# A two-layer encoder on one core: the pick of modulations one chunk behind its row product, the first sums in one piece, a constant loaded later

## The chip, the cores and the metric

The kernel runs on one core of a Trainium2 chip. The metric is the device time of one execution in microseconds (us), and less is better. The engines are TensorE (PE, whose weight loads are listed as PEld), VectorE (DVE), ScalarE (ACT), GpSimd (POOL) and SyncE (SP, which issues nearly all DMAs). Each works through its own queue in order, and waits on the others through semaphores.

## What is computed

A trunk of two residual layers over x of 1024 tokens x 1024 features, conditioned by a vector c, all in float32. The reference, cut to what matters here:

```
ada = silu(c) @ ada_w[l] + ada_b[l]          # 3 x 1024: shift, scale, gate
h   = rms_norm(x, norm_g[l]) * (1 + scale) + shift
x   = x + gate * mixer_l(h)

mixer 0: proj = h @ w_in -> q, k, v, g_a, x_b, g_b
         a = diff_attention(q, k, v) with
             lam = exp(sum(lp[0]*lp[1])) - exp(sum(lp[2]*lp[3])) + lam_init
         b = bidir_rglru(x_b)
         out = concat([a * silu(g_a), b * silu(g_b)]) @ w_out
mixer 1: neighbourhood attention over the token grid, 16 heads, with gate and w_out
```

After both layers comes a final RMSNorm. What matters here is small beside the rest: shift, scale and gate ("the modulations", ada above), the sum of squares and 1/sqrt of each norm, and the scalar lam.

## The kernel before

Features lie on the 128 partitions and tokens along the free axis. So an activation is 8 tiles (k = 0 to 7) of 128 x 1024, and each is worked on in two halves of 512 tokens (hf = 0, 1; HF = 512). A product with weights takes three passes in a reduced format: weight and activation are each split in a high and a low part (whi, wlo; ahi, alo or yhi, ylo), and `mm3` issues hi x hi, hi x lo, lo x hi (L204 to L206). One output chunk of `proj` is 8 k x 3 = 24 matmuls of 128 x 512 into one PSUM bank. Weight slabs of 512 KB (raw) are loaded by SP, split by ACT (whi, L187) and POOL (wlo = raw - whi, L188); slab i + 1 is split when chunk i has been issued.

**PSUM.** Pool pp has two banks, pool ps two and pool pt two. While `wide` is on, the chunks take pp, pp, ps, ps in turn. A row product (below) takes a bank of pp too.

**A norm.** ACT or DVE squares the tiles. `ss_add` multiplies a tile by a block of ones and adds up over partitions in a bank, `rstd_rows` (L388 to L394) makes 1/sqrt on DVE: rs, rr, then three rounds of three small operations. `spread` (L407) copies the result to all partitions by four matmuls (tile bc, or the bank norm0, norm1 at the start). `make_h` multiplies the tile by gain and 1/sqrt (L414), makes its high part on ACT (L415) and its low part on DVE (L416).

**The start.** The tiles xT, the first slabs and four sets of ada pieces (8 pieces of 256 KB each) come through SP's queue in one stream. `squares(hf)` loads and squares one half; `mod_first(g)` makes shift and scale of tiles 2g and 2g + 1: 32 small matmuls ("sums", L281, tile mod) over the 8 pieces, a copy of the row on ACT (L304), the pick (L306, a matmul that puts the row's numbers on partitions), then first and gain on DVE (L310, L312). `scale(hf)` runs `rstd_rows` and `spread` at high priority and copies the spread bank to SBUF (bcs, L555); `parts(g, hf)` calls make_h for two tiles, `products` multiplies them with the first three slabs. The constant lam is made in `small_constants` ahead of all this: its load (lpv, 128 x 256 float32, L504) stands third in SP's queue.

**The changeover** is the output projection of layer 0 (`out_layer(0, ...)`). Segment r0 does eight chunks for the first half of the tokens (weight slabs 24 to 31, tiles pp24_0 to pp31_0), r1 the same for the second half (pp32_1 on). Behind each chunk, `evac` on DVE adds gate x chunk to the residual tile (xh, L1149, at high priority), ACT squares it (L1154), and DVE adds the square to the running sum (sq, L1160). `tail(0)` is the norm of the first half: ssl, rs, rr, rt, spread.

Beside this run the modulations of layer 1, a generator `mod_part` per 512 of them. DVE adds up eight pieces of ada_w times c in a tile macc (L342, then seven of L344), with a yield after each. Then follow three empty yields, the row product (L378, tile mrow, by `ss_add`), ACT's copy of the row (L356), the pick (L361, held behind the last matmul issued so far) and the addition of ada_b on DVE (L366, mod1). The loop steps this generator three times behind each chunk (`after_dve`), and it runs over two parts in a row, so the second part's additions begin behind the first part's L366.

The order on each engine is that in which the code issues, apart from `high_priority` and `issue_after`, by which the scheduler places an instruction earlier, or behind a named one.

Of the kernel before, what the change touches and what calls it, by code (L numbers as in the profile page):

```python
# [15 lines left out]
ALU = mybir.AluOpType  # L16
# [81 lines left out]
def kernel(ctx, tc, xT, xTp, small, lamp, adaw, tb, w0, gw, wo0, w1, nab, wo1, out):  # L98
# [175 lines left out]
    def mod_first(g, pool, small, c32):  # L274
# [31 lines left out]
        T.matmul(pc[:, :4], row[:], pick[:], start=True, stop=True)  # L306
# [10 lines left out]
    def mod_part(l, t, part, pool, tag="ada", bufs=2, acc=None, wait=3, apart=False,  # L317
                 early=False):
# [39 lines left out]
        if apart:  # L358
            yield 0.0
# [49 lines left out]
    def make_h(l, k, hf, x, bc):  # L409

        g, b = first_mod[k] if l == 0 else (gain1[:, k:k + 1], modc[1][:, k:k + 1])
        hi = actp.tile([P, HF], F32R, tag=f"hi{k}_{hf}", name=f"ahi{k}_{hf}")
        lo = actp.tile([P, HF], F32R, tag=f"lo{k}_{hf}", name=f"alo{k}_{hf}")
        V.scalar_tensor_tensor(x, x, g, bc, ALU.mult, ALU.mult)  # L414
        A.activation(hi[:], x, AF.Identity, bias=b)  # L415
        V.scalar_tensor_tensor(lo[:], x, b, hi[:], ALU.add, ALU.subtract)  # L416
        hact[k, hf] = (hi, lo)
# [55 lines left out]
    def small_constants(lp):  # L473
# [27 lines left out]

        lpm = lp.tile([P, 2, 64], F32, tag="lpm", name="lpm", bufs=1)
# [10 lines left out]
    with tc.tile_pool(name="start", bufs=2) as stp, tc.tile_pool(name="ada0", bufs=KC) as adp:  # L513
# [12 lines left out]
        def squares(hf, on_dve, pool, tag):  # L526
# [5 lines left out]
            for k in range(KC):  # L532
                sq = stp.tile([P, HF], F32, tag="sq", name="sq", bufs=SQ)
                if k in on_dve:
                    V.tensor_tensor(sq[:], half(k, hf), half(k, hf), ALU.mult)
                else:
                    A.activation(sq[:], half(k, hf), AF.Square)
                sqs.append(sq)
                if hf == 0:
                    ss_add(ss, sq, k == 0, k == KC - 1)  # L540
# [8 lines left out]
        def scale(hf):  # L549

            with tc.high_priority():
                rr = rstd_rows(nbank[hf], D, stp)
                spread(rr, nbank[hf])
                bcs[hf] = stp.tile([P, HF], F32, tag="bcs", name="bcs")
                A.activation(bcs[hf][:], nbank[hf][:], AF.Copy)  # L555

        def parts(g, hf):
            for k in (2 * g, 2 * g + 1):
                make_h(0, k, hf, half(k, hf), bcs[hf][:])
# [39 lines left out]
        for g in range(1, KC // 2):  # L599
            if g == 1:  # L600
                with tc.issue_after(state["x"].ins):
                    mod_first(3, adp, stp, c32)
            for hf in range(2):
                parts(g, hf)
# [610 lines left out]
    with tc.tile_pool(name="bound", bufs=2) as bp:  # L1215
# [4 lines left out]
        mod = mods(NM[2], bp, bufs=4, wait=NW[2])  # L1220
# [361 lines left out]
```

## Time and profile before

| what | us |
|---|---|
| median of three runs | 1188.19 |
| lowest, highest run | 1186.65, 1191.43 |
| the profiled execution's own time | 1190.72 |
| its span in the trace | 1189.0 |
| PE busy | 1145.3 (96%) |
| DVE, ACT, POOL busy | 738.1, 560.3, 371.8 |

The busy times come from one profiled execution, on one core; they overlap, so they don't add up to the span. PE is the engine that is nearly always at work. "Granted clock" or PEclk is the share of full speed (2.4 GHz) that PE was given in a stretch; 0.50 is the lower level, 1.2 GHz. In a timeline, a row with "x8" groups eight instructions that follow each other, and the number in brackets is the idle time of that engine just before, with what ended it.

### The profile page before, as it was taken

The numbers are of one execution on the slowest core, as the hardware profiler recorded it, in microseconds if no ns is written. First come the engines' busy times: TensorE is split into PE (matmuls) and PEld (weight loads), VectorE is DVE, ScalarE is ACT, GpSimd is POOL, SyncE is SP. The second block draws the span as 40 slices with busy tenths as digits, with TensorE's granted clock in tenths as the row PEclk, the third lists the DMA queues.
The fourth block names the chain that finished last, engine by engine and source line by source line (L and its number), as shares of the span: only waits on it lengthen the run. The fifth ranks groups of instructions, "written<-read, shape, count | busy, mean of one in ns | idle before, by whom it ended". The sixth has DMA issues, their size and how long they took to land.

```text
span 1189.0 us, 19211 instructions
## 1 busy us (share of the span) xinstructions
PE 1145.3 (96%) x7232; PEld 975.3 (82%) x7232; DVE 738.1 (62%) x1422; ACT 560.3 (47%) x1029; POOL 371.8 (31%) x346
## 2 busy tenths in 40 slices
PE   5999999999999999999999999999999999999997
PEld 2788777888887888777878888988998998888896
DVE  6857959699888979778663344233434443555454
ACT  4357685475655657432442444344444434446121
POOL 2124322233333332343422433332333333316100
PEclk8999999999999999999999999999999999999998
DMA  9723131432122112485513433243453534314212
GB/s 325 240 80 125 36 140 53 142 90 78 36 87 63 32 39 71 145 283 183 185 46 123 139 111 91 85 134 110 129 172 88 162 126 117 93 35 156 98 72 71
DMA packets 85789, 136.46 MB, mean 115 GB/s; under 512 B 8000, under 2 KB 49472, under 8 KB 85696
## 3 DMA queue, kind: packets, MB, share of 16 engines
q1 hardware_dynamic: 85696, 135.23, 36.3%
q8 instruction: 57, 0.93, 0.3%
q14 instruction: 36, 0.29, 0.1%
HBM read 112.13 MB, written 16.78 MB: 108 GB/s over the span
## 4 chain that ended last, share of the span: by engine, by line
PE 74%; DVE 13%; ACT 5%; DMA 4%; issue 3%; POOL 1%; SPq 0%; DVEq 0%; POOLq 0%; ACTq 0%
PE pp L204 14%; PE pp L205 14%; PE pp L206 14%; PE no L1418 4%; PE etr L1400 3%; PE v L204 2%; PE v L206 2%; PE v L205 2%; PE n L671 2%; DVE e L1003 2%; PE atr L1033 2%; PE n L672 2%; PE s L671 1%; PE s L672 1%; DMA ada<-in_adaw_dram 1%
## 5 line engine op out<-in xcount | busy, mean ns | idle before, releaser
L204 PE MATMUL pp<-ahi,whi 128*128 128x512 f32 (+1 forms) x976 | 370.8, 380 | 2.0 <-DVE sgb L677 1.8
L206 PE MATMUL pp<-ahi,wlo 128*128 128x512 f32 (+1 forms) x976 | 367.9, 377 | 1.1 <-POOL wlo L188 1.1
L205 PE MATMUL pp<-alo,whi 128*128 128x512 f32 (+1 forms) x976 | 368.6, 378 | 0.0
L188 POOL TENSOR_TENSOR wlo<-raw,whi 128x1024 fp32r<-128x1024 f32 x80 | 197.0, 2465 | 260.9 <-ACT whi L187 242.2
L206 PEld LDWEIGHTS pp<-ahi,wlo 128*128 128x128 f32 x976 | 184.0, 189 | 35.5 <-POOL wlo L188 1.6
L204 PEld LDWEIGHTS pp<-ahi,whi 128*128 128x128 f32 x976 | 184.3, 189 | 34.8 <-DVE sgb L677 2.3
L205 PEld LDWEIGHTS pp<-alo,whi 128*128 128x128 f32 x976 | 184.3, 189 | 30.8 <-issue 0.2
L1389 POOL TENSOR_SCALAR e<-e,r 128x288 f32<-128x288 f32 (+1 forms) x128 | 71.2, 569 | 235.9 <-DVE r L1387 229.7
L187 ACT ACTIVATE whi<-raw 128x1024 fp32r<-128x1024 f32 x80 | 84.3, 1056 | 107.1 <-PE pp L205 52.7
L1007 ACT ACTIVATE e<-e,nm 128x1024 f32<-128x1024 f32 x64 | 73.6, 1151 | 46.6 <-DVE nm L1003 46.3
L1384 ACT ACTIVATE e<-e,nm 128x288 f32<-128x288 f32 (+1 forms) x128 | 72.7, 569 | 47.2 <-DVE nm L1381 40.4
L1406 DVE COPY e<-etr 96x384 f32<-96x384 f32 (+1 forms) x64 | 35.5, 554 | 94.2 <-PE etr L1400 91.5
L1381 DVE CUSTOM_DVE_ANT_0 e<-n,bias 128x288 f32<-128x288 f32 (+1 forms) x128 | 60.6, 504 | 45.5 <-PE n L672 33.0
L1404 ACT ACTIVATE e<-etr 96x384 f32<-96x384 f32 (+1 forms) x64 | 31.3, 489 | 117.8 <-DVE e L1406 117.4
L1003 DVE CUSTOM_DVE_ANT_0 e<-s,tb 128x1024 f32<-128x1024 f32 x64 | 77.3, 1218 | 6.4 <-PE s L672 4.9
L1024 POOL TENSOR_SCALAR e<-e,r 128x256 f32<-128x256 f32 x32 | 32.6, 1018 | 131.8 <-DVE r L1013 73.7
L204 PE MATMUL v<-whi,ahi 128*128 128x256 f32 x256 | 72.2, 282 | 0.0
L206 PE MATMUL v<-whi,alo 128*128 128x256 f32 x256 | 71.9, 281 | 0.0
L205 PE MATMUL v<-wlo,ahi 128*128 128x256 f32 x256 | 71.9, 281 | 0.0
L1040 ACT ACTIVATE ath<-atr 128x512 fp32r<-128x512 f32 x64 | 37.5, 596 | 39.7 <-PE atr L1033 39.4
L1400 PE MATMUL etr<-ident,e 128*96 128x128 f32 (+1 forms) x384 | 52.3, 272 | 0.5 <-POOL e L1389 0.5
L671 PE MATMUL s<-ks,qq 128*128 128x512 f32 x128 | 52.5, 410 | 0.0
(218 smaller groups left out, 2111.3 us busy)
## 6 DMA issues: line engine op xcount, KB each, us to landing
raw<-in_w_dram SPq DMA_DIRECT2D x56, 512.0 KB
ada<-in_adaw_dram SPq DMA_DIRECT2D x96, 256.0 KB
raw<-in_wo_dram SPq DMA_DIRECT2D x24, 512.0 KB
bias<-in_nab_dram SPq DMA_DIRECT2D x64, 144.0 KB
qq<-qq SPq DMA_DIRECT2D x48, 128.0 KB
bias<-in_nab_dram SPq DMA_DIRECT2D x32, 192.0 KB
xT<-in_xT_dram SPq DMA_DIRECT2D x16, 256.0 KB
vd<-vt SPq DMA_DIRECT2D x32, 128.0 KB
```

The lines of the kernel that those rows point to most:

```text
L187: A.activation(hi[:], raw[:], AF.Copy)
L188: G.tensor_tensor(lo[:], raw[:], hi[:], ALU.subtract)
L204: T.matmul(ps, lh, rh, start=start, stop=False)
L205: T.matmul(ps, lh, rl, start=False, stop=False)
L206: state["pe"] = T.matmul(ps, ll, rh, start=False, stop=stop).ins
L671: T.matmul(dst, qsel(q[m]), k, start=True, stop=False)
L1003: state["dve"] = V.tensor_tensor_reduce(out=e[:], in0=ps[:].rearrange("p a b -> p (a b)"), in1=tbt["tb"][:, o:o + S], scale=-1.0, scalar=3 ...
L1007: A.activation(e[:], e[:], AF.Exp, scale=-1.0, bias=nm[:], accum_out=sums[:, m:m + 1])
L1381: state["dve"] = V.tensor_tensor_reduce(out=e[:, m, :n], in0=ps[:, m, :n], in1=bias["now"][m][:, :n], scale=-1.0, scalar=3.0e38, op0=ALU.a ...
L1384: A.activation(e[:, m, :n], e[:, m, :n], AF.Exp, scale=-1.0, bias=nm[:, m:m + 1], accum_out=sums[:, m:m + 1])
L1389: state["pool"] = G.tensor_scalar(e[:, m, :n], e[:, m, :n], r[:, m:m + 1], 0.0, ALU.mult, ALU.add).ins
L1400: T.transpose(pt[:kn, m, j * P:(j + 1) * P], e[:, m, j * kn:(j + 1) * kn], ident[:])
```

## The change

Five edits, one at the changeover and four at the start:

1. `mod_part` gets `gap`, a number of empty yields between ACT's copy of the row and the pick. The modulations at the changeover use gap=3, which is one chunk's worth of steps.
2. At the start, the spread of the first half is issued behind the first pick (`state["picked"]`), so the 32 first sums stand in front of it.
3. The constant lam moves to a function of its own, `lam_constant`, called behind the loads of the fourth set of ada pieces.
4. make_h for the first two tiles of each half reads 1/sqrt from the spread's PSUM bank (`nbank`) in place of the SBUF copy bcs.
5. The squares of the second half are issued behind the last alo (`state["lo"]`) of the first two tiles.

```diff
@@ mod_first @@
-        T.matmul(pc[:, :4], row[:], pick[:], start=True, stop=True)
+        state["picked"] = T.matmul(pc[:, :4], row[:], pick[:], start=True, stop=True).ins
@@ mod_part @@
-                 early=False):
+                 early=False, gap=0):
...
-        if apart:
+
+        for _ in range(1 if apart else gap):
             yield 0.0
         with tc.issue_after(state["pe"]):
             T.matmul(pc[:, :4], row, pick[:], start=True, stop=True)
@@ make_h @@
-        V.scalar_tensor_tensor(lo[:], x, b, hi[:], ALU.add, ALU.subtract)
+        state["lo"] = V.scalar_tensor_tensor(lo[:], x, b, hi[:], ALU.add, ALU.subtract).ins
@@ small_constants, split in two @@
+    def lam_constant(lp):
+
         lpm = lp.tile([P, 2, 64], F32, tag="lpm", name="lpm", bufs=1)
         lpv = lp.tile([P, 256], F32, tag="lpv", name="lpv", bufs=1)
         nc.sync.dma_start(lpv[:], lamp)
@@ squares @@
-                if k in on_dve:
-                    V.tensor_tensor(sq[:], half(k, hf), half(k, hf), ALU.mult)
-                else:
-                    A.activation(sq[:], half(k, hf), AF.Square)
+
+                with tc.issue_after(state["lo"]) if hf else nullcontext():
+                    if k in on_dve:
+                        V.tensor_tensor(sq[:], half(k, hf), half(k, hf), ALU.mult)
+                    else:
+                        A.activation(sq[:], half(k, hf), AF.Square)
@@ scale @@
-                spread(rr, nbank[hf])
+                with nullcontext() if hf else tc.issue_after(state["picked"]):
+                    spread(rr, nbank[hf])
@@ parts @@
-                make_h(0, k, hf, half(k, hf), bcs[hf][:])
+
+                make_h(0, k, hf, half(k, hf), bcs[hf][:] if g else nbank[hf][:])
@@ the loop over groups at the start @@
                     mod_first(3, adp, stp, c32)
+                    lam_constant(stp)
@@ the changeover @@
-        mod = mods(NM[2], bp, bufs=4, wait=NW[2])
+        mod = mods(NM[2], bp, bufs=4, wait=NW[2], gap=3)
```

Lines below the edits move by up to nine in the changed file, so L361 becomes L362, L1149 becomes L1158, and so on. The orders below are those of the built programs.

**PE at the start**, before and then after: norm is the bank of the first half's squares and spread, mod that of the first sums, start the first products.

```order
L378 MATMUL norm_190<-sq,ones 32x128 x32
L281 MATMUL mod_239<-ada,c_126 32x128 x20
L407 MATMUL norm_190<-rr,sel 128x128 x4
L281 MATMUL mod_239<-ada,c_126 32x128 x12
L306 MATMUL mod_239<-pick,mrow 128x4
L573 MATMUL start_450<-ahi_0_321,whi_295 128x512
```
```order
L379 MATMUL norm_181<-sq,ones 32x128 x32
L281 MATMUL mod_230<-ada,c_126 32x128 x32
L306 MATMUL mod_230<-pick,mrow 128x4
L408 MATMUL norm_181<-rr,sel 128x128 x4
L581 MATMUL start_441<-ahi_0_312,whi_286 128x512
```
The spread (rr, sel) has moved from behind 20 of the 32 sums to behind all of them and the pick.

**PE at the changeover**, before: the row product mrow, the first matmuls of chunk 30 and the pick.

```order
L378 MATMUL mrow_5163<-macc_4950,ones_90 32x128 x4
L204 MATMUL pp30_0_5180<-yhi0_0_4540,whi30_5157 128x512
L205 MATMUL pp30_0_5180<-ylo0_0_4542,whi30_5157 128x512
L206 MATMUL pp30_0_5180<-yhi0_0_4540,wlo30_5158 128x512
L204 MATMUL pp30_0_5180<-yhi1_0_4544,whi30_5157 128x512
L361 MATMUL mrow_5163<-pick_94,macc_4950 128x4
L205 MATMUL pp30_0_5180<-ylo1_0_4546,whi30_5157 128x512
L206 MATMUL pp30_0_5180<-yhi1_0_4544,wlo30_5158 128x512
```
After: the last matmuls of chunk 30, the pick and the first of chunk 31.

```order
L206 MATMUL pp30_0_5171<-ahi2_0_4891,wlo30_5158 128x512
L204 MATMUL pp30_0_5171<-ahi3_0_4895,whi30_5157 128x512
L205 MATMUL pp30_0_5171<-alo3_0_4896,whi30_5157 128x512
L206 MATMUL pp30_0_5171<-ahi3_0_4895,wlo30_5158 128x512
L362 MATMUL mrow_5163<-pick_94,macc_4950 128x4
L204 MATMUL pp31_0_5216<-yhi0_0_4540,whi31_5201 128x512
L205 MATMUL pp31_0_5216<-ylo0_0_4542,whi31_5201 128x512
```
The pick has moved from behind chunk 30's fourth matmul to behind its 24th, just ahead of chunk 31.

**DVE at the changeover**, before: xh are the evacuations of chunks 29, 30 and 31, sq the running sum of squares, mod1 the reader of the pick, macc the additions of the next part.

```order
L1149 SCALAR_TENSOR_TENSOR xh0_0_5_5087<-pp29_0_5127,mod0_101,xh0_0_5_5087 128x512
L366 TENSOR_TENSOR mod1_102<-mrow_5163,sm_85 128x4
L342 TENSOR_SCALAR macc_5171<-ada_5172,ctmp_97 128x512
L1160 TENSOR_TENSOR sq_5154<-sq_5154,sq_5116 128x512
L344 SCALAR_TENSOR_TENSOR macc_5171<-ada_5175,ctmp_97,macc_5171 128x512
L1149 SCALAR_TENSOR_TENSOR xh0_0_6_5125<-pp30_0_5180,mod0_101,xh0_0_6_5125 128x512
L344 SCALAR_TENSOR_TENSOR macc_5171<-ada_5216,ctmp_97,macc_5171 128x512
L1160 TENSOR_TENSOR sq_5207<-sq_5207,sq_5154 128x512
L344 SCALAR_TENSOR_TENSOR macc_5171<-ada_5219,ctmp_97,macc_5171 128x512
L344 SCALAR_TENSOR_TENSOR macc_5171<-ada_5222,ctmp_97,macc_5171 128x512
L1149 SCALAR_TENSOR_TENSOR xh0_0_7_5178<-pp31_0_5225,mod0_101,xh0_0_7_5178 128x512
```
After:

```order
L1158 SCALAR_TENSOR_TENSOR xh0_0_5_5087<-pp29_0_5127,mod0_101,xh0_0_5_5087 128x512
L1169 TENSOR_TENSOR sq_5154<-sq_5154,sq_5116 128x512
L1158 SCALAR_TENSOR_TENSOR xh0_0_6_5125<-pp30_0_5171,mod0_101,xh0_0_6_5125 128x512
L367 TENSOR_TENSOR mod1_102<-mrow_5163,sm_85 128x4
L342 TENSOR_SCALAR macc_5209<-ada_5210,ctmp_97 128x512
L344 SCALAR_TENSOR_TENSOR macc_5209<-ada_5213,ctmp_97,macc_5209 128x512
L1169 TENSOR_TENSOR sq_5198<-sq_5198,sq_5154 128x512
L1158 SCALAR_TENSOR_TENSOR xh0_0_7_5169<-pp31_0_5216,mod0_101,xh0_0_7_5169 128x512
```
The reader of the pick and the first two additions have moved behind the evacuation of chunk 30; the third to fifth have moved behind that of chunk 31.

**DVE from the evacuation of chunk 31 to the first norm's chain**, before: rs, rr and rt are the steps of 1/sqrt.

```order
L1149 SCALAR_TENSOR_TENSOR xh0_0_7_5178<-pp31_0_5225,mod0_101,xh0_0_7_5178 128x512
L344 SCALAR_TENSOR_TENSOR macc_5171<-ada_5261,ctmp_97,macc_5171 128x512
L1160 TENSOR_TENSOR sq_5252<-sq_5252,sq_5207 128x512
L344 SCALAR_TENSOR_TENSOR macc_5171<-ada_5264,ctmp_97,macc_5171 128x512
L344 SCALAR_TENSOR_TENSOR macc_5171<-ada_5267,ctmp_97,macc_5171 128x512
L1149 SCALAR_TENSOR_TENSOR xh0_1_0_5270<-pp32_1_5274,mod0_101,xh0_1_0_5270 128x512
L388 TENSOR_SCALAR rs_5314<-ssl0_0_5309 128x128
L389 TENSOR_SCALAR rr_5315<-rs_5314 128x128
L392 SCALAR_TENSOR_TENSOR rt_5316<-rr_5315 128x128
```
After:

```order
L1158 SCALAR_TENSOR_TENSOR xh0_0_7_5169<-pp31_0_5216,mod0_101,xh0_0_7_5169 128x512
L344 SCALAR_TENSOR_TENSOR macc_5209<-ada_5252,ctmp_97,macc_5209 128x512
L1169 TENSOR_TENSOR sq_5243<-sq_5243,sq_5198 128x512
L344 SCALAR_TENSOR_TENSOR macc_5209<-ada_5255,ctmp_97,macc_5209 128x512
L344 SCALAR_TENSOR_TENSOR macc_5209<-ada_5258,ctmp_97,macc_5209 128x512
L344 SCALAR_TENSOR_TENSOR macc_5209<-ada_5300,ctmp_97,macc_5209 128x512
L344 SCALAR_TENSOR_TENSOR macc_5209<-ada_5303,ctmp_97,macc_5209 128x512
L1158 SCALAR_TENSOR_TENSOR xh0_1_0_5261<-pp32_1_5265,mod0_101,xh0_1_0_5261 128x512
L389 TENSOR_SCALAR rs_5314<-ssl0_0_5309 128x128
L390 TENSOR_SCALAR rr_5315<-rs_5314 128x128
L344 SCALAR_TENSOR_TENSOR macc_5209<-ada_5306,ctmp_97,macc_5209 128x512
L393 SCALAR_TENSOR_TENSOR rt_5316<-rr_5315 128x128
```
Between the two evacuations of chunks 31 and 32 stand five additions where there were three, and the eighth has moved in between rr and rt.

## Rows read from the trace of the kernel before

**Rows 1.** The page: busy time, share and instructions of each engine, whole span.
```profile
PE 1145.3 (96%) x7232; PEld 975.3 (82%) x7232; DVE 738.1 (62%) x1422; ACT 560.3 (47%) x1029; POOL 371.8 (31%) x346
```

**Rows 2.** Timeline at the changeover: start, length, engine, line, operation, [idle before <-releaser].
```profile
529.76 0.40 PE L204 MATMUL pp<-yhi,whi 128*128 128x512 f32 x1
...
531.64 1.06 ACT L187 ACTIVATE whi<-raw 128x1024 fp32r<-128x1024 f32 x1 [4.86 <-DMA raw<-in_wo_dram]
...
532.60 0.26 ACT L356 ACTIVATE macc<-mrow 128x128 f32<-128x128 f32 x1
...
532.76 0.62 ACT L1154 ACTIVATE sq<-xh 128x512 f32<-128x512 f32 x1
...
532.77 2.36 POOL L188 TENSOR_TENSOR wlo<-raw,whi 128x1024 fp32r<-128x1024 f32 x1 [4.11 <-ACT whi L187]
...
532.91 0.59 PE L361 MATMUL mrow<-pick,macc 128*128 128x4 f32 x2 [2.75 <-ACT macc L356]
...
535.34 0.68 DVE L1160 TENSOR_TENSOR sq<-sq 128x512 f32<-128x512 f32 x1
...
540.69 0.39 PE L204 MATMUL pp<-yhi,whi 128*128 128x512 f32 x1
...
540.89 0.75 DVE L1149 SCALAR_TENSOR_TENSOR xh<-pp,mod,xh 128x512 f32<-128x512 f32 x1 [4.21 <-PE pp L206]
```

**Rows 3.** Windows: length, busy us by engine, clock (PEclk), DMA share, GB/s.
```profile
532.91:539.08 6.17, 6.17 (x16) 4.91 (x17) 3.14 (x4) 0.47 (x1) 2.23 (x1) 0.50 1.01 377
...
545.00:551.00 6.00, 6.00 (x28) 4.99 (x27) 5.93 (x7) 1.69 (x2) 2.84 (x1) 1.00 0.52 177
...
378.70:382.10 3.40, 3.40 (x14) 3.30 (x15) 1.89 (x4) 0.50 (x1) 1.97 (x3) 0.50 0.51 169
```

**Rows 4.** Timeline from chunk 31's last matmul to the spread of the next norm.
```profile
545.90 0.39 PE L206 MATMUL pp<-ahi,wlo 128*128 128x512 f32 x1
...
547.91 2.77 DVE L1160 TENSOR_TENSOR sq<-sq 128x512 f32<-128x512 f32 x1
...
550.60 1.53 DVE L344 SCALAR_TENSOR_TENSOR macc<-ada,ctmp,macc 128x512 f32<-128x512 f32 x2
...
552.73 2.40 POOL L188 TENSOR_TENSOR wlo<-raw,whi 128x1024 fp32r<-128x1024 f32 x1 [2.60 <-ACT whi L187]
...
553.02 2.18 DVE L389 TENSOR_SCALAR rr<-rs 128x128 int32<-128x128 int32 x1
...
555.24 0.29 DVE L392 SCALAR_TENSOR_TENSOR rt<-rr 128x128 f32<-128x128 f32 x1
...
557.85 0.29 DVE L394 SCALAR_TENSOR_TENSOR rr<-rt,rr 128x128 f32<-128x128 f32 x1
...
558.20 1.16 PE L407 MATMUL bc<-rr,sel 128*128 128x128 f32 x8
...
558.75 2.38 POOL L188 TENSOR_TENSOR wlo<-raw,whi 128x1024 fp32r<-128x1024 f32 x1 [3.63 <-ACT whi L187]
```

**Rows 5.** Timeline: a spread in layer 0's attention that waited for its chain.
```profile
378.63 0.58 PE L407 MATMUL obc<-osq,sel 128*128 128x128 f32 x1 [1.98 <-DVE osq L394]
```

**Rows 6.** Timeline, PE at the start: spreads, first sums, pick, first product.
```profile
18.59 1.13 PE L407 MATMUL norm<-rr,sel 128*128 128x128 f32 x8 [1.28 <-DVE rr L394]
...
20.91 0.39 PE L306 MATMUL mod<-pick,mrow 128*128 128x4 f32 x2 [0.40 <-ACT mrow L304]
...
33.52 1.95 PE L281 MATMUL mod<-ada,c 128*32 128x128 f32 x64
...
35.63 1.16 PE L407 MATMUL norm<-rr,sel 128*128 128x128 f32 x8
...
38.89 0.50 PE L573 MATMUL start<-ahi,whi 128*128 128x512 f32 x1 [1.99 <-ACT ahi L415]
```

**Rows 7.** Windows at the start, columns as in rows 3.
```profile
33.30:36.00 2.70, 2.55 (x69) 2.06 (x68) 2.05 (x7) 0.28 (x1) 0.00 (x0) 1.00 1.09 347
...
38.90:44.00 5.10, 5.10 (x77) 3.84 (x77) 5.10 (x9) 3.17 (x5) 0.00 (x0) 1.00 1.10 349
```


## The prediction

> **What bounds the kernel now.** The page comes first: TensorE (PE) is busy for 1145.3 of 1189.0 us [rows 1], so an edit is worth only what it takes from PE's pauses or adds to them, and from the half-clock stretches that follow some of them. The diff touches two places. For each I read the timeline around it, PE's idle time in brackets first, then the windows for the granted clock.
>
> Place one is the branch's changeover, the out-projection of layer 0. PE starts the fourth matmul of chunk 30 at 529.76 and then idles 2.75 us until the pick of modulations at 532.91. The pick needs ACT's copy of the row product. That copy (L356, 532.60) stands in ACT's queue behind whi of the next weight slab (531.64 to 532.70), which came late [rows 2]. After the pause the clock is granted at 0.50, the lower level: in 532.91 to 539.08 PE does 16 matmuls in 6.17 us, 0.386 each. At full clock they start 0.227 apart: chunk 31's 24 go from 540.69 to 545.90, which is 23 steps [rows 2 to 4]. The slow stretch costs 6.17 - 16 x 0.227 = 2.5 us, with the pause 5.3. That is the prize.
>
> Place two is the start. The first sums on PE are cut by rstd's spread at 18.59, and the pick stands behind the rest of them at 20.91 [rows 6]. All of this lies under the load stream: the DMA engines' share is 1.09 in 33.3 to 36.0, at 347 GB/s [rows 7].
>
> **The start, part by part.** Putting all 32 sums and the pick ahead of the spread brings the pick forward by about the spread's 1.13 us, at most by 20.91 - 18.59 = 2.3. Reading rstd's rows from PSUM drops bcs's copy from the path. I take the first products to come 1 to 1.7 us earlier. Who takes that up? The second modulation's 64 sums start at 33.52 and the spread follows at 35.63 [rows 6]; PE's queue goes on behind them. The sums need the last of their eight loads, in a stream that is full. Nothing that PE or DVE does earlier shortens that stream, except that the constant's load (lpv, 131 KB) leaves its place ahead of xT for one behind the fourth set of ada: 0.131 MB at 347 GB/s is 0.38 us. I take **0.45 us** of gain (loads that wait for a buffer may start a little earlier too); bounds 0 (another load is late) and 1.7 (the whole gain passes through). The constant's five small operations, four of them on DVE, now stand among the work of the third group. None is longer than a full addition of 0.77 (two take 1.53 [rows 4]); I take nothing for them, since DVE's alo tiles behind them are read by PE only after the other products of their group; without that cover they would cost up to 3.1. The squares of the second half start later, behind the first alo; their sums wait for the last of the same loads, so I take nothing, and up to one square, 0.77, if not.
>
> **The changeover, step by step.** Times stay on the axis of before. In the changed order the pick stands behind all 24 matmuls of chunk 30. The other 20 follow at full clock, so the pick's place comes at 529.76 + 21 x 0.227 = 534.5. The copy is done at 532.86; the pick waits for nothing. Next stands pp31's first matmul, possible at 534.75. But pool pp has two banks; one holds the row (freed by DVE's L366), the other chunk 30 (freed by DVE's evacuation L1149). On DVE, L366 has moved behind that evacuation. Whichever of the banks pp31 gets, it waits for the evacuation of chunk 30. Before, chunk 31 started at 540.69 while that evacuation began at 540.89 [rows 2]. And ahead of the evacuation stands a sum of squares (L1160), whose operands all lie in SBUF.
>
> That matters, since the rows show such a DVE operation standing still for as long as a POOL split (L188) runs: rr takes 2.18 us from 553.02 with POOL busy from 552.73 to 555.13, and L1160 takes 2.77 at 547.91 against 0.68 at 535.34 [rows 2, 4]. In the new order L1160 is ready at 533.4 (its square on ACT runs from 532.76 for 0.62), just after POOL's split began (532.77 to 535.13). It ends at about 535.65, the evacuation at 536.4, and **pp31 starts at 536.42**, after 1.6 us of idle and 4.27 us ahead of 540.69. Bounds of this term: 5.94 us if nothing waits (534.75), and 4.27 - 2.5 = 1.8 if the new pause brings a half-clock stretch as the old one did.
>
> The Trainium skill has a rule that speaks against this order: "Perfetto Trace Analysis", section on matmuls, wants independent groups of matmuls to rotate through different PSUM banks, so that the evacuation of one overlaps the matmuls of the next. The trace before agrees (540.69 against 540.89); the edit breaks it by keeping the row in one of two banks. With the rule kept, pp31 would start at 534.75 and the sum be 1.67 us better.
>
> **What is late next: the spread of the next norm.** Call P the start of chunk 31's last matmul: 545.90 before, 536.42 + 23 x 0.227 = 541.7 after. ACT's whi waits for slabs that PE gives back and POOL's splits wait for whi, so these keep their distance from P: 552.73 is P+6.8 and 558.75 is P+12.85. Before, DVE's rstd chain (rs, rr, then nine operations, 0.326 apart from 555.24 to 557.85) ends at 558.14, although rr was held for two us; PE reaches the spread at 558.20 = P+12.3 and loses next to nothing, and the next split starts 0.6 us later [rows 4].
>
> In the changed order DVE has more to do there. The row sum of the next modulations is eight additions of 0.77 each; it begins behind chunk 30's evacuation instead of in the pause, and so six of them instead of three stand behind chunk 31's evacuation, the last inside the rstd chain, behind rr. I walk it: evacuation of chunk 31 from P+0.4, an addition from 1.1, the sum of squares held by POOL until about 4.6 (before, 547.91 + 2.77 = P+4.8), four additions until 7.65, the next evacuation until 8.4, rs, rr until about 9.5 (the split of P+6.8 ends at 9.2), the last addition until 10.3, and nine operations would end at 13.2. At P+12.85 POOL's next split begins, and what is left of the chain stands until P+15.2. The spread goes at **P+15.4**, PE idles some 3.2 us. If the fourth of those additions (ready at P+6.88) also falls under the split of P+6.82, which is a hair's breadth, all is about 1.15 later: P+16.55, idle 4.4. If the chain slips through, the spread goes at P+13.4, idle 1.2.
>
> An idle of this size can also move the clock. After the 2.75 us at 532.91 came 6.17 us at 0.50; after 1.98 us at 378.63 came 3.40 us at 0.50 [rows 2, 3, 5]. After 1.99 us at 38.89 none came [rows 6, 7]. A half-clock stretch of 3.4 us costs 1.7, one of 6.2 some 2.5.
>
> **The sum**, against the profiled execution's 1190.72 us: start -0.45; pp31 earlier -4.27; idle at the spread +3.2; its half clock +1.7: **+0.2, some 1190.9**. With the fourth addition caught too: -0.45 - 4.27 + 4.4 + 2.5 = +2.2, some 1192.9. The profiled execution lies 2.53 above the median of the runs shown (1188.19, from 1186.65 to 1191.43). If that surplus lies elsewhere, these are 1188.4 and 1190.4 on the median's scale; if it is the pause that is removed, the times stand as they are. The middle of the four is 1190.6; the first case is the likelier of the two, so I take **1190.0**.
>
> **The rivals.**
> - The chain slips through: POOL's split starts later, or DVE gets on faster. For it: before, the chain missed the split by 0.6 us. Against it: about 1 us more stands ahead of its end. -0.45 - 4.27 + 1.2 = -3.5: 1187.2, or 1184.7 on the median's scale.
> - The pauses vanish: pp31 finds a bank free at once and the chain is through in time. -0.45 - 5.94 = -6.4: 1184.3 or 1181.8. Against it: DVE's order, and DVE is already busy for 5.93 of 6.00 us in 545 to 551 [rows 3].
> - The start keeps more: another wait than the stream sets 33.52, and 1.7 us pass through: 0.2 - 1.25 = -1.0: 1189.7 or 1187.1. Against it: the DMA share of 1.09 [rows 7].
> - **Slower**: both new pauses throw the clock down. The 1.6 us ahead of pp31 bring a stretch as the old 2.75 did (+2.5), on top of the case with both additions and chain caught: +2.2 + 2.5 = +4.7: 1195.4 or 1192.9. It decides when the pause ahead of pp31 is long enough to lower the clock; 1.98 us was once and 1.99 was not [rows 5, 6], so 1.6 is on the mild side.
> - The edit does nothing at the changeover: the pick's place behind 24 matmuls is in the order itself, and its copy ends 1.6 us ahead of that place. I give it no chance of its own.
>
> **Chances.** Forecast (the chain caught, with or without the addition) 0.58; slips through 0.18; the pauses vanish 0.09; the start keeps more 0.08; slower 0.07. The range reaches to the slipped chain and into the slower case: 1184.5 to 1194.0. What lies outside is most of the vanished pauses, half of the slower case, and some spread of the runs, together under 0.2. A measurement of this kernel can tell about 0.5%, 5.9 us, from no change. Faster by that are the vanished pauses alone, 0.09; slower by that the last rival, 0.07; within it 0.84.
>
> **What would show it.** In the changed profile: the pick directly behind chunk 30's 24th matmul, without a wait; pp31 some 0.5 to 2 us later, waiting for L1149, with an L1160 of over 2 us in front; no half clock there. Then, at the spread of the next norm (L407), an idle of 1 to 4.5 us released by rr (L394), with one operation of the chain over 2 us long, and 0.50 behind it. At the start, the second modulation's sums within 0.5 us of 33.5. Wrong would be: pp31 without a wait, or the chain done before PE arrives (the time then falls by 3 to 6 us), or the second modulation's sums a full 1 us earlier.

## The result, and the profile after

| | before | after |
|---|---|---|
| median, us | 1188.38 (8 runs) | 1193.17 (8 runs) |
| lowest, highest | 1185.11, 1191.97 | 1192.44, 1195.38 |
| profiled execution's own time | 1190.72 | 1192.76 |
| span in the trace | 1189.0 | 1191.0 |

The ratio after to before is 1.0044, with a 95% interval of 1.0027 to 1.006. The change costs about 5 us, and the interval is clear of no change. The two profiled executions differ by only 2.0 us; why the runs differ by more is looked at below.

The page's line of busy times, as in [rows 1]: PE is busy 1.6 us longer, and the span grew by 2.0.

```profile
PE 1146.9 (96%) x7232; PEld 977.1 (82%) x7232; DVE 737.9 (62%) x1422; ACT 560.4 (47%) x1029; POOL 371.6 (31%) x346
```

**The changeover.** The timeline of after, answering to [rows 2] (columns: start, length, engine, line, operation, idle before and its releaser):

```profile
528.87 1.06 ACT L187 ACTIVATE whi<-raw 128x1024 fp32r<-128x1024 f32 x1 [3.24 <-DMA raw<-in_wo_dram]
...
529.84 0.26 ACT L356 ACTIVATE macc<-mrow 128x128 f32<-128x128 f32 x1
...
530.01 2.39 POOL L188 TENSOR_TENSOR wlo<-raw,whi 128x1024 fp32r<-128x1024 f32 x1 [2.54 <-ACT whi L187]
...
530.65 2.30 DVE L1169 TENSOR_TENSOR sq<-sq 128x512 f32<-128x512 f32 x1 [1.97 <-ACT sq L1163]
...
533.41 0.28 PE L362 MATMUL mrow<-pick,macc 128*128 128x4 f32 x2
...
533.61 0.75 DVE L1158 SCALAR_TENSOR_TENSOR xh<-pp,mod,xh 128x512 f32<-128x512 f32 x1 [0.65 <-PE pp L206]
...
534.41 0.50 PE L204 MATMUL pp<-yhi,whi 128*128 128x512 f32 x1 [0.73 <-DVE xh L1158]
```

The copy of the row is done at 530.1, the pick at 533.41 has no bracket: it waits for nothing. The sum of squares (L1169) is held for 2.30 us while POOL splits (530.01 to 532.40). It ends early enough, the evacuation of chunk 30 follows its own matmuls, and chunk 31 pauses 0.73 us for that evacuation (L1158). The windows, answering to [rows 3], show no half clock behind this pause, but one behind the next (columns: length, busy us of PE, PEld, DVE, ACT, POOL, clock, DMA share, GB/s):

```profile
534.40:540.00 5.60, 5.59 (x25) 4.62 (x26) 3.79 (x4) 0.62 (x2) 2.51 (x1) 1.00 0.98 344
...
556.20:561.40 5.20, 5.20 (x17) 4.61 (x18) 3.44 (x8) 1.84 (x3) 0.00 (x0) 0.50 0.46 151
```

**The spread of the next norm**, rows of DVE, POOL and PE in this order of time, answering to [rows 4]:

```profile
539.76 0.39 PE L206 MATMUL pp<-ahi,wlo 128*128 128x512 f32 x1
...
544.32 5.21 DVE L344 SCALAR_TENSOR_TENSOR macc<-ada,ctmp,macc 128x512 f32<-128x512 f32 x4
...
546.59 2.40 POOL L188 TENSOR_TENSOR wlo<-raw,whi 128x1024 fp32r<-128x1024 f32 x1 [2.74 <-ACT whi L187]
...
550.56 0.75 DVE L344 SCALAR_TENSOR_TENSOR macc<-ada,ctmp,macc 128x512 f32<-128x512 f32 x1
...
552.61 2.40 POOL L188 TENSOR_TENSOR wlo<-raw,whi 128x1024 fp32r<-128x1024 f32 x1 [3.63 <-ACT whi L187]
...
552.85 2.31 DVE L395 SCALAR_TENSOR_TENSOR rr<-rt,rr 128x128 f32<-128x128 f32 x1
...
556.19 2.08 PE L408 MATMUL bc<-rr,sel 128*128 128x128 f32 x8 [4.22 <-DVE rr L395]
```

Chunk 31's last matmul is at 539.76. Behind it come four additions that take 5.21 us in place of 3.1, since POOL's split of 546.59 holds one of them. The eighth addition stands at 550.56 between rr and rt. The next split begins at 552.61, and the sixth of the chain's nine operations, at 552.85, takes 2.31 us in place of 0.29. PE stands 4.22 us at the spread, released by the chain's last operation, and then works at 0.50 for 5.2 us, as the second window showed.

**The start**, PE rows of after, answering to [rows 6]:

```profile
23.07 0.80 PE L581 MATMUL start<-ahi,whi 128*128 128x512 f32 x1 [2.22 <-ACT ahi L416]
...
32.51 1.95 PE L281 MATMUL mod<-ada,c 128*32 128x128 f32 x64 [0.20 <-DMA ada<-in_adaw_dram]
...
41.60 2.48 PE L281 MATMUL mod<-ada,c 128*32 128x128 f32 x64
...
48.55 1.95 PE L281 MATMUL mod<-ada,c 128*32 128x128 f32 x64
```

and two rows of before for the third and fourth set of first sums, which were not shown yet:

```profile
42.05 1.96 PE L281 MATMUL mod<-ada,c 128*32 128x128 f32 x64
...
48.56 1.95 PE L281 MATMUL mod<-ada,c 128*32 128x128 f32 x64
```

The first product comes 0.2 us earlier than before (23.07 against 23.28), the second set of sums 1.0 us earlier (32.51 against 33.52), the third 0.45, the fourth 0.01. The gain is gone before the start is over. It goes in a stretch of half clock that before does not have (window of after, columns as above):

```profile
39.30:42.70 3.40, 3.40 (x30) 2.34 (x32) 3.40 (x6) 1.85 (x3) 0.00 (x0) 0.50 1.10 348
```

Ahead of it PE paused 1.99 us (up to the product at 37.66). Before had the same pause, up to 38.89, and kept the full clock behind it [rows 6, 7].

I set the n-th of PE's 7232 matmuls in one trace against the n-th in the other. After minus before: -1.25 us at 40.6, 0.00 at 48.8, -0.05 from 107 to 342, -1.14 from 397 to 515, -6.15 behind chunk 31's start, +0.53 behind the spread, +2.14 from 644 on. What is gained at the start goes between 40.6 and 42.5, in the half clock shown above. The step between 342 and 397 lies at 380, behind a pause of 1.97 us at a spread in layer 0's attention; in before it was 1.98 with half clock behind it [rows 3, 5], in after there was none. The step up to 644 lies behind a pause of 2.15 us at 632 in layer 1 (1.91 before), with a half-clock stretch behind it in after alone. Neither place is near an edit. **The changeover alone, from 515 to 584, costs 1.67 us in this pair of traces**: 5.01 gained at the pick, 6.68 lost at the spread.

### The profile page after: what moved, and what is told of

Same layout as the page of the kernel before. It is cut to its first block, busy times and chain, and to the rows that moved or that the text cites. A ratio compares the mean times of both kernels' runs of the same rounds, so it can differ in the third digit from the quotient of the medians.

```text
span 1191.0 us, 19214 instructions
## 1 busy us (share of the span) xinstructions
PE 1146.9 (96%) x7232; PEld 977.1 (82%) x7232; DVE 737.9 (62%) x1422; ACT 560.4 (47%) x1029; POOL 371.6 (31%) x346
## 4 chain that ended last, share of the span: by engine, by line
PE 76%; DVE 11%; ACT 4%; DMA 4%; issue 2%; POOL 1%; SPq 0%; DVEq 0%; POOLq 0%; ACTq 0%
PE pp L204 15%; PE pp L205 15%; PE pp L206 15%; PE no L1427 4%; PE etr L1409 3%; PE v L204 2%; PE v L206 2%; PE v L205 2%; PE n L680 2%; DVE e L1012 2%; PE atr L1042 2%; PE n L681 2%; PE s L680 1%; PE s L681 1%; DMA raw<-in_w_dram 1%
## 5 line engine op out<-in xcount | busy, mean ns | idle before, releaser
L344 DVE SCALAR_TENSOR_TENSOR macc<-ada,ctmp,macc 128x512 f32<-128x512 f32 x56 | 52.0, 929 | 6.6 <-DMA ada<-in_adaw_dram 6.2
L1163 ACT ACTIVATE sq<-xh 128x512 f32<-128x512 f32 (+1 forms) x37 | 19.9, 537 | 73.6 <-DVE xh L1158 72.7
```

The source lines that it names most:

```text
L344: V.scalar_tensor_tensor(acc[:], piece[:], ctmp[:, k:k + 1], acc[:], ALU.mult, ALU.add)
```

## Experiments

Two questions were open: which part of the change loses, and why the pair of traces shows a smaller loss than the runs. Theory A was that of the prediction: the additions pushed behind chunk 31 put the rstd chain under POOL's split. Its rivals: B, the start loses; C, the old pause at the pick is a draw that most executions don't have; D, the pick's new place hurts in itself (the held bank, the loads); E, something behind the spread is late anyway.

### Each half of the change alone

c_gap3 is the kernel before with the first edit alone:

```diff
-        if apart:
+        for _ in range(1 if apart else gap):
             yield 0.0
...
-        mod = mods(NM[2], bp, bufs=4, wait=NW[2])
+        mod = mods(NM[2], bp, bufs=4, wait=NW[2], gap=3)
```

> The kernel before with gap=3 at the changeover alone; the start is as before. Theory A (the loss is made at the changeover: six of the eight additions now stand behind chunk 31, the rstd chain of the next norm is caught by POOL's split, and PE idles at the spread): ratio 1.002 to 1.006; the spread some 16.5 us behind chunk 31's last matmul, after an idle of about 4.2 us released by the chain, with the granted clock near 0.5 behind it. Theory B (the loss is made at the start, by loads that come in another order): ratio 0.997 to 1.001.

Measured: 1193.97 us, ratio 1.0044 (1.0028 to 1.006). PE at chunk 31 and at the spread:

```profile
537.01 0.50 PE L204 MATMUL pp<-yhi,whi 128*128 128x512 f32 x1 [0.73 <-DVE xh L1149]
...
558.79 2.08 PE L407 MATMUL bc<-rr,sel 128*128 128x128 f32 x8 [4.22 <-DVE rr L394]
...
558.80:562.10 3.30, 3.30 (x13) 3.11 (x14) 1.54 (x5) 0.63 (x1) 0.00 (x0) 0.50 0.54 186
```

The same two pauses as in after, to 0.01 us, and by the runs the whole loss is there with the old start. The half clock behind the second pause is shorter (the window: 3.3 us, in after 5.2 and a little more), so this trace loses 0.68 us across the changeover, that of after 1.67.

s_start is the changed kernel with the first edit undone:

```diff
-        mod = mods(NM[2], bp, bufs=4, wait=NW[2], gap=3)
+        mod = mods(NM[2], bp, bufs=4, wait=NW[2])
```

> The changed kernel with gap=0: the four edits at the start alone. Theory A: ratio 0.999 to 1.001; the first products come 1.2 us earlier, and by the fourth set of first sums (48.6 us) nothing of it is left. Theory B: ratio 1.003 to 1.005, with sums of the third or fourth set later than before.

Measured: 1186.91 us, ratio 0.9986 (0.9972 to 0.9999). The fourth set of first sums:

```profile
47.19 1.96 PE L281 MATMUL mod<-ada,c 128*32 128x128 f32 x64
```

Theory B falls: the start doesn't lose. It wins 1.7 us, with an interval from 0.1 to 3.3. The expectation missed all the same. The first products were to come 1.2 us earlier and came 0.16 earlier (23.12); by the fourth set nothing was to be left, and that set comes 1.37 us ahead of before. This trace has no half clock near 40 us, so the loads let the third and fourth set come that early. In the traces, at PE's 700th matmul (107 us), the nine traces with the new start stand between 1.3 us ahead of before and 2.2 behind, 0.3 behind on the mean; the four others with the old start, and before itself, 0.5 behind on the mean. So the start's gain is of the size of its scatter there. Much of this scatter is the clock: eight of the nine traces with the new start have a half-clock stretch that begins between 38.1 and 40.2 us, all but s_start, and of the five with the old start only c_gap3 and w_only have one.

### The pause at the pick is a draw

n_before is the kernel before, unchanged, against itself; n_before2 and s_start2 are one more execution each of it and of s_start. These two, n_before, s_start and the trace of before share the order at the changeover.

> The kernel before against itself: ratio 0.998 to 1.002, and a second profile. If the pause at the pick hangs on when the weight slab lands (rival C), it differs from 2.75 us here, and the time differs by that and by its half-clock stretch; if it is a fixed part of the kernel, it is within 0.5 us of 2.75.

> The kernel before once more, one look. If the pause at the pick is fixed: 2.6 to 2.8 us again. If it hangs on the landing of one weight slab (rival C): it may be anything from 0.4 to 2.8, with the half clock behind it only if it is long, and the time goes with it.

> The four edits at the start alone once more, one look. Its first look had 0.4 us at the pick, with the same order at the changeover as the kernel before. If the new start itself removes the pause: 0.4 again. If the pause is a draw (rival C): it may be 2.7 as well.

Measured: n_before 1188.16 us, ratio 0.9997 (0.9979 to 1.0015). The pick on PE and the window behind it, n_before:

```profile
533.72 0.59 PE L361 MATMUL mrow<-pick,macc 128*128 128x4 f32 x2 [2.59 <-ACT macc L356]
...
533.72:539.90 6.18, 6.18 (x16) 4.92 (x17) 3.15 (x4) 0.46 (x1) 2.23 (x1) 0.50 1.03 392
```

n_before2:

```profile
533.67 0.39 PE L361 MATMUL mrow<-pick,macc 128*128 128x4 f32 x2 [1.54 <-ACT macc L356]
...
533.67:537.00 3.33, 3.33 (x16) 2.80 (x17) 2.91 (x4) 0.47 (x1) 2.25 (x1) 1.00 1.04 406
```

s_start:

```profile
529.81 0.39 PE L362 MATMUL mrow<-pick,macc 128*128 128x4 f32 x2 [0.40 <-ACT macc L356]
...
529.81:533.20 3.39, 3.39 (x16) 2.88 (x17) 2.96 (x4) 0.47 (x1) 2.25 (x1) 1.00 1.04 404
```

s_start2:

```profile
532.90 0.39 PE L362 MATMUL mrow<-pick,macc 128*128 128x4 f32 x2 [1.75 <-ACT macc L356]
...
533.74:537.15 3.41, 3.41 (x10) 2.64 (x9) 2.94 (x3) 0.00 (x0) 1.40 (x1) 0.50 1.05 402
```

With [rows 2] these are five pauses at one place of one order: 2.75, 2.59, 1.54, 0.40 and 1.75 us. In each the copy of the row stands behind ACT's whi, and whi waits for the DMA of its slab. n_before alone would have spoken for a fixed pause, as its expectation puts it (2.59 is within 0.5 of 2.75); the other three show the draw. Behind the two long pauses came some 6.2 us at 0.50, behind 1.75 us came 3.4 (from 533.74, 0.8 us after the pick), behind 1.54 and 0.40 none. The shift of PE's matmuls across the changeover (515 to 584), against the trace of before, is 0, -0.09, -4.08, -5.25 and -2.23 us; mean -2.33. So the trace of before showed nearly the worst draw. Rival C holds in a milder form: the pause is common, but its cost is between 0 and 5.3 us, some 3 on the mean of these five. Whether the new start shortens it, five traces can't tell: it is 2.75, 2.59 and 1.54 with the old start, 0.40 and 1.75 with the new one.

That narrows the gap between traces and runs, and doesn't quite close it. Against the mean of the five, the changeover of after costs 1.67 + 2.33 = 4.0 us, and c_gap3's 0.68 + 2.33 = 3.0; the runs say 4.8 and 5.3, with intervals of 3.2 to 7.1 and 3.3 to 7.1. An estimate from the other side: c_gap3 and w_only (below) differ from before at the changeover alone, and their traces stand 0.68 us behind and 5.49 ahead of the trace of before there. If these two traces are typical, their runs (5.3 us slower, 1.3 faster) ask that the average execution of before stand some 4.6 (2.6 to 6.4) and 4.2 us (2.5 to 5.9) ahead of that trace, about as n_before2 does with 4.08. The old pause would then cost the average execution some 1 us, not 3.

The profiled execution of before stood 2.53 us above its median, that of n_before 2.91, and both have the long pause. That the pause was the surplus is likely but not shown: the profiled executions of a_steps5 and b_late (below) stand 2.2 and 3.4 us above their medians without a pause at the pick.

### The additions behind chunk 31

a_steps5 keeps gap=3, but steps the modulations faster behind the last two chunks:

```diff
-            after_dve(mod, 3)
+            after_dve(mod, 3 if c < 6 else 5)
```

> The changed kernel, with five steps of the modulations in place of three behind the last two chunks of the first half: the pick keeps its new place, but four additions instead of six stand behind chunk 31's evacuation, and none inside the rstd chain. Theory A (the additions push the chain under POOL's split): the third addition ends just ahead of one split, the chain ends about 0.4 us ahead of the next, the pause at the spread falls from 4.2 to below 0.5 us, and the ratio to 0.995 to 0.999. Rival D (the pause comes from something else that the pick's new place does, such as the bank or the loads): the pause stays above 2 us and the ratio at 1.003 to 1.006.

Measured: 1186.6 us, ratio 0.9995 (0.998 to 1.001). Rows of DVE, POOL and PE near the spread:

```profile
546.88 2.31 DVE L344 SCALAR_TENSOR_TENSOR macc<-ada,ctmp,macc 128x512 f32<-128x512 f32 x3
...
549.14 2.40 POOL L188 TENSOR_TENSOR wlo<-raw,whi 128x1024 fp32r<-128x1024 f32 x1 [2.74 <-ACT whi L187]
...
550.08 1.54 DVE L390 TENSOR_SCALAR rr<-rs 128x128 int32<-128x128 int32 x1
...
554.27 0.29 DVE L395 SCALAR_TENSOR_TENSOR rr<-rt,rr 128x128 f32<-128x128 f32 x1
...
554.62 1.16 PE L408 MATMUL bc<-rr,sel 128*128 128x128 f32 x8
...
555.16 2.39 POOL L188 TENSOR_TENSOR wlo<-raw,whi 128x1024 fp32r<-128x1024 f32 x1 [3.62 <-ACT whi L187]
```

Three additions behind the sum of squares end at 549.2, as the split of 549.14 begins; none is held (2.31 us for three). rr is held until 551.6 (1.54), the chain ends at 554.56, 0.6 us ahead of the next split, and the spread goes at 554.62 with no pause. Two additions fewer behind chunk 31, with the pick in its new place, and the loss is gone. Rival D falls. The gain over before that was expected (0.995 to 0.999) is not there beyond the interval; chunk 31 paused 1.21 us here for the evacuation of chunk 30, against 0.73 in after.

g_gap2 is the other way round: gap=2 leaves the pick behind the fourth matmul of chunk 30, but delays the additions.

```diff
-        mod = mods(NM[2], bp, bufs=4, wait=NW[2], gap=3)
+        mod = mods(NM[2], bp, bufs=4, wait=NW[2], gap=2)
```

> The changed kernel with gap=2 in place of 3: the pick is back behind the fourth matmul of chunk 30, as before, while five additions (before three, with gap=3 six) stand behind chunk 31's evacuation. Theory A: a pause at the spread of 3 to 4 us with the half clock behind it, although the pick has its old place; a pause at the pick of 0.4 to 2.8 us as before; ratio 1.003 to 1.008. Rival D: no pause at the spread above 1 us, ratio 0.998 to 1.001.

Measured: 1193.98 us, ratio 1.006 (1.0038 to 1.0081). Rows at the pick and near the spread:

```profile
531.85 0.39 PE L362 MATMUL mrow<-pick,macc 128*128 128x4 f32 x2 [1.26 <-ACT macc L356]
...
554.82 2.34 POOL L188 TENSOR_TENSOR wlo<-raw,whi 128x1024 fp32r<-128x1024 f32 x1 [3.63 <-ACT whi L187]
...
554.85 2.46 DVE L393 SCALAR_TENSOR_TENSOR rt<-rr 128x128 f32<-128x128 f32 x1
...
558.01 2.08 PE L408 MATMUL bc<-rr,sel 128*128 128x128 f32 x8 [3.83 <-DVE rr L395]
```

The pick has its old place and its old pause (1.26 this time), and the spread pauses 3.83 us because the seventh operation of the chain, ready at 554.85, met a split that began at 554.82. Theory A's pause is there without the pick's move.

### The held bank

p_ptbank is the changed kernel with the first row product in pool pt:

```diff
-        if apart:
+        if apart or (gap and part == 0):
             ps = ptp.tile([P, HF], F32, tag="pt", name="mrow")
```

> The changed kernel with the first row product in a bank of pool pt, so that it holds none of the two banks that the chunks use there. Theory A: chunk 31 starts without the pause of 0.7 us, and all the rest stays: the pause of 4.2 us at the spread, ratio 1.003 to 1.005. Rival D (the held bank is what hurts): pause at the spread below 2 us and ratio below 1.001.

Measured: 1192.22 us, ratio 1.0037 (1.002 to 1.0054). Chunk 31's first matmul, chunk 30's evacuation and the spread:

```profile
535.59 0.48 PE L204 MATMUL pp<-yhi,whi 128*128 128x512 f32 x1
...
536.45 0.74 DVE L1158 SCALAR_TENSOR_TENSOR xh<-pp,mod,xh 128x512 f32<-128x512 f32 x1
...
557.45 1.55 PE L408 MATMUL bc<-rr,sel 128*128 128x128 f32 x8 [4.31 <-DVE rr L395]
```

Chunk 31 starts at 535.59 without a bracket, 0.86 us ahead of chunk 30's evacuation, so the pause of 0.73 us did come from the bank. The time doesn't show it beyond its interval, and the pause at the spread is 4.31: rival D falls here too. The Trainium skill's rule in "Perfetto Trace Analysis", section on matmuls, that independent groups should rotate through different PSUM banks, is borne out by this trace: with the row in another pool's bank the pause of 0.73 us is gone.

### The spread one chunk later

l_late is the changed kernel with the spread, and all steps behind it, issued one chunk later:

```diff
-            some(t0, (1, 1, 2, 2, 2, 2, 0, 0)[c])
+            some(t0, (1, 0, 1, 2, 2, 2, 2, 0)[c])
```

> The changed kernel with the spread of the first half issued one chunk later (behind chunk 34 in place of 33), all else as it is: DVE's order up to the end of the rstd chain and POOL's splits stay. Theory A (the chain is late, and PE stands at the spread because the spread is next in its queue): the chain still has an operation of over 2 us, the spread finds it done, no pause above 0.5 us, ratio 0.995 to 0.999. Rival E (something behind the spread needs it at once): the pause moves to a later place of PE and the ratio stays above 1.002.

Measured: 1187.74 us, ratio 0.9994 (0.9981 to 1.0008). POOL, DVE and PE:

```profile
554.48 2.46 POOL L188 TENSOR_TENSOR wlo<-raw,whi 128x1024 fp32r<-128x1024 f32 x1 [3.63 <-ACT whi L187]
...
554.72 2.37 DVE L395 SCALAR_TENSOR_TENSOR rr<-rt,rr 128x128 f32<-128x128 f32 x1
...
557.77 0.29 DVE L395 SCALAR_TENSOR_TENSOR rr<-rt,rr 128x128 f32<-128x128 f32 x1
...
559.57 1.05 PE L408 MATMUL bc<-rr,sel 128*128 128x128 f32 x8
...
577.99 0.50 PE L206 MATMUL pp<-yhi,wlo 128*128 128x512 f32 x1 [0.58 <-POOL wlo L188]
```

The chain is caught as in after (2.37 us under the split of 554.48) and ends at 558.06. But PE does chunk 34 meanwhile and reaches the spread at 559.57 without a pause. So the lost time is PE's wait at the spread. Of rival E a small rest is left: a pause of 0.58 us at 577.99, for a low part of the weights (wlo) from POOL, which only this trace and b_late's have; it costs 0.85 us. The ratio is just above the expected band (0.995 to 0.999), and far below rival E's 1.002. Rival E falls as the cause of the loss.

### A version without either pause

v_wait4 is the changed kernel with wait=4 beside gap=3: the row product comes one chunk earlier, and the pick stands behind chunk 29's last matmul, four matmuls ahead of its old place. DVE's order is that of before, but for one sum of squares that changes places with an addition ahead of chunk 30's evacuation. w_only is the same edit on the kernel before, b_late is v_wait4 with l_late's edit.

```diff
-        mod = mods(NM[2], bp, bufs=4, wait=NW[2], gap=3)
+        mod = mods(NM[2], bp, bufs=4, wait=4, gap=3)
```

> The changed kernel, but with wait=4 in place of 7 beside gap=3: the row product comes one chunk earlier (ahead of chunk 29), the pick stays behind chunk 29, and DVE's order at the changeover is that of the kernel before. Theory A: no pause at the pick, no pause at the spread (below 0.5 us), ratio 0.994 to 0.998. Rival C (the pause of 2.75 us at the pick was a rare draw of one late weight slab, most executions have none): the same trace, ratio 0.999 to 1.001.

> The kernel before with wait=4 and gap=3 at the changeover, the start as before: the row product one chunk earlier, DVE's order as before. If the two halves of the better version add up (0.9961 with the new start, the start alone 0.9986): ratio 0.996 to 0.999, no pause at the pick or at the spread. If the start alone carried it: 0.999 to 1.001.

> The version with wait=4 and gap=3 and the new start, with the spread one chunk later as well. There the chain ends at about the time at which PE arrives, so the later spread should win nothing: ratio 0.995 to 0.998, as without it (0.9961). If a small wait at the spread is still paid there, 0.5 us less.

Measured: v_wait4 1184.58 us, ratio 0.9961 (0.9944 to 0.9977); w_only 1186.25, 0.9989 (0.9975 to 1.0003); b_late 1187.45, 0.9991 (0.998 to 1.0001). The pick and the spread on PE in v_wait4:

```profile
530.43 0.28 PE L362 MATMUL mrow<-pick,macc 128*128 128x4 f32 x2
...
553.63 1.16 PE L408 MATMUL bc<-rr,sel 128*128 128x128 f32 x8
```

No bracket at either. Across the changeover v_wait4, w_only and b_late stand 5.53, 5.49 and 4.75 us ahead of the trace of before, thus 2.4 to 3.2 ahead of the mean of the five draws. v_wait4's 4.6 us (2.7 to 6.7) agree with that plus a little from the start. w_only's 1.3 (up to 3.0) is at the lower edge, on the border of its two expected cases. b_late's expectation missed: it was to be like v_wait4 and was 3.6 us slower against its own runs of before. Its trace doesn't explain that: it is the slowest of its executions (1190.81 us, median 1187.45), and lost 2.24 us by the 700th matmul, most of it in a half-clock stretch at 33.4 to 36.7 us that no other trace has. v_wait4 was measured on another chip than the other two. Which of the three is the typical size stays open. That v_wait4 beats both kernels is measured, once; w_only and b_late are not told from before.

## Why the prediction held, and where it was off

The forecast was no measurable change, at 1190.0 us, between 1184.5 and 1194.0. Measured were 1193.17 us, 0.44% above before (0.27 to 0.6%), inside the 0.5% and inside the range, but in its upper part. The loss is clear of the scatter all the same: from median to median the forecast was +1.8 us, the runs gave +4.8. Step by step:

- **The pick waits for nothing.** Right: no bracket at 533.41.
- **Chunk 31 waits for the evacuation, with a held sum of squares in front.** Right in kind: released by L1158, and L1169 took 2.30 us. Off in size: 0.73 us in place of 1.6. The walk took whi's time over from the trace of before (531.64), which was the late draw; in after whi of that slab began at 528.87. p_ptbank showed the bank as the cause.
- **No half clock there.** Right; the slower rival, which needed one, did not happen.
- **The rstd chain is caught by POOL's split.** Right, and in the worse form: the fourth addition was held too. The spread went 16.43 us behind chunk 31's last matmul (556.19 - 539.76), forecast 16.55; PE stood 4.22 us, forecast 4.4; the half-clock stretch was 5.2 us long and a little more (3.3 in c_gap3 behind the same pause), forecast 3.4 to 6.2. The first of the two cases, with 15.4, was taken for the likelier; the other one came in after, c_gap3 and p_ptbank. The additions are ready within 0.1 us of the split's start, so the walk by hand could not decide it. g_gap2 and a_steps5 showed from both sides that the count of additions behind chunk 31's evacuation sets it: with five the chain is caught, with four it is not.
- **The start wins 0.45 us.** Right in outcome: s_start 1.7 us (0.1 to 3.3), traces 0.2 on the mean (0.5 against 0.3 us behind). Wrong in the step, so the outcome is luck: the first products came 0.2 us earlier and not 1 to 1.7, and the load stream did not hold back the second set of sums (it came 1.0 us earlier, where "a full 1 us" was named as a sign of error). What took the gain back in after was the clock, 0.50 in 39.30 to 42.70 behind a pause that was there before too. Where that stretch is missing, in s_start's trace, 1.3 us pass through: the fourth set comes at 47.19.
- **The scale of the sum.** Here the number went wrong. Profile against profile the worse case gave +2.2, some 1192.9; measured were +2.0 and 1192.76. This agreement is in part luck, since the +2.0 holds draws of -1.09 and +1.61 us at places that no edit touches; the changeover's part was forecast as +2.6 and came to +1.67. The profiled execution of before stood 2.53 us above its median, and the text left open whether that surplus was the pause to be removed. The long pauses of before and n_before speak for it. Then "the times stand as they are", 1190.9 or 1192.9, and the median came to 1193.17. The middle of four, 1190.6, and the step from it to 1190.0 were the mistake: the gain of 4.27 at the pick was priced from a trace with nearly the longest pause, and the mean execution had less to win, some 2.3 us by the five traces and some 4 by the runs of c_gap3 and w_only.

Every held operation of 0.29 us here took 2.31 to 2.46 and ended with POOL's split of 2.34 to 2.46, while the evacuations, which read one input from PSUM, took 0.74 or 0.75 throughout, under a split too (a_steps5, 549.11, with the split of 549.14). DVE's stalls are so as the Trainium skill has them in "SBUF — State Buffer", section on the two separate sides: VectorE and GpSimd share one pair of ports under an exclusive lock, which a VectorE operation with two inputs in SBUF needs against a GpSimd one that reads SBUF, and the loser waits for the whole instruction.

## What to carry to other kernels

When a late operand stalls PE, produce it earlier; moving its reader later (gap) also moves everything that the reader's generator issues behind it. Here that was eight additions of 0.77 us, three of which moved behind chunk 31's evacuation and so pushed a chain that PE waits for under another engine's split; earlier production (wait=4) all but kept DVE's order and took both pauses away. And before a pause is booked as a gain, find out whether it is a draw: two more traces of the kernel before showed 2.59 and 1.54 us in place of 2.75, and one more alone might have misled.

## What the runs showed of the hardware

The same pause does not always cost the same clock. A pause of 1.82 to 1.86 us in layer 0's projections, at some 205 us, stands in all fourteen traces, and no edit is near it. In after:

```profile
204.81 0.50 PE L204 MATMUL pp<-ahi,whi 128*128 128x512 f32 x1 [1.84 <-DVE sgb L686]
...
204.85:208.25 3.40, 3.40 (x15) 2.81 (x16) 2.58 (x4) 1.23 (x2) 0.00 (x0) 1.00 0.23 88
```

In v_wait4:

```profile
205.17 0.51 PE L204 MATMUL pp<-ahi,whi 128*128 128x512 f32 x1 [1.84 <-DVE sgb L686]
...
206.60:210.00 3.40, 3.40 (x10) 2.63 (x9) 1.91 (x4) 1.23 (x2) 0.00 (x0) 0.50 0.68 240
```

Eleven of the fourteen traces have a half-clock stretch there, as v_wait4 (0.50 over 3.40 us, from 206.60, and some 1.6 us lost on PE), while before, n_before and after have none. At the spread near 380 us, with a pause of 1.96 to 2.00, before, n_before and n_before2 have a half-clock stretch, and the other eleven have none. At the start, behind the pause of 1.99 or 2.00 us that after has up to 37.66 and before up to 38.89, ten of the fourteen have one; before, n_before, n_before2 and s_start have none. So a single trace carries several such draws, of one to two us each in either direction, and the -1.09 at 380 and the +1.61 at 632 of the pair above are two of them; what decides the draw was not tried.
